# Interleaving the two halves of the split activations in the down projection of a decoder layer

## The chip, the cores and the metric

The kernel runs on one core of a Trainium2 chip. The metric is the device time of one execution in microseconds; the time of a kernel is the median over its runs. TensorE (PE) multiplies: a weight load puts a stationary operand of 128 x 128 into its array, and a matmul then streams a moving operand past it and accumulates into PSUM. VectorE (DVE), ScalarE (ACT) and GpSimd (POOL) work on elements; SyncE (SP) issues most transfers. All operands lie in SBUF, 128 partitions wide; what is said below of steps in bytes is within a partition.

## The reference

One decoder layer on 256 tokens of width 2048 in float32: a token mixer (mLSTM and RWKV-7 side by side), a cross-attention into 256 memory tokens, and a channel mixer, each with an RMS norm before and after and a residual. The change lies in the channel mixer:

```python
def conv_glu_ffn(h, w_up, conv_w, conv_b, w_down):
    u = h @ w_up
    uc = conv_b + sum(conv_w[j] * shift_right(u, CONV_WIDTH - 1 - j) for j in range(CONV_WIDTH))
    gate, up = split_cols(uc, (D_FF, D_FF))
    return (jax.nn.gelu(gate, approximate=True) * up) @ w_down
```

D_FF is 8192, so the last product is (256 x 8192) by (8192 x 2048). It is the last stage of the kernel, before the final norm and residual.

## The kernel before, in words

**Two halves for precision.** TensorE multiplies faster in the rounded type fp32r than in float32. To keep float32 accuracy each operand is split: the high half is the value rounded to fp32r, the low half is what the rounding left. A product is three matmuls: high x high, low x high, high x low. The weights arrive by DMA as pieces of 512 KB (128 x 1024 words, the tile `raw`); ScalarE casts a piece into `wh` (line 391) and VectorE subtracts to get `wl` (line 421). The class `Feed` (line 345) keeps these three steps ahead of the matmuls by fixed distances, with four buffers for each tile. Activations are split by the helper `split` (line 232), a cast on ScalarE and a subtraction on VectorE; through a recording wrapper these instructions all show line 66 in the profile. All matmuls but the transposes are issued at line 181.

**Two kinds of stage.** In an "fm" stage the weights are stationary and the activations move, 256 columns (all tokens) per matmul. In a "tm" stage the activations are stationary, 128 tokens at a time, and the weights move, 512 columns per matmul. The up projection is "fm" (32 blocks of 512 columns, line 1870). The down projection, the stage of the change, is "tm" (line 2006): two blocks n of 1024 output columns each, and for each block 64 steps k over D_FF, 128 rows of w_fd at a time. One k is one weight piece. For each k the four PSUM banks of a block (two halves of the tokens by two halves of the 1024 columns) get three matmuls each, twelve per k and 2 x 64 x 12 = 1536 in all, each with a weight load of its own:

```python
    def tm_products(o, t, c, wx, first, last):
        ...
        mm(o, xh[:, t], wh[:, c], start=first, stop=False)
        mm(o, xl[:, t], wh[:, c], start=False, stop=False)
        mm(o, xh[:, t], wl[:, c], start=False, stop=last)
```

Here `xh` and `xl` are the halves of the activations of one k, 128 x 256 words each, and `t` picks 128 of the 256 tokens.

**Where the halves come from.** The gated activations wait in SBUF as 64 tiles `ac` (`actile`, line 1816). `asplit` (line 1879) splits two of them, k and k + 1, into one tile `as` of 1024 words per partition. Two such tiles take turns (tags au0 and au1), the last pair has a third (bg0). `ax` (line 1894) hands the halves to the matmuls and calls `asplit` one pair ahead: while pair n is multiplied, pair n + 1 is split into the buffer that pair n - 1 has left. So the first cast of a pair waits for the matmuls of the pair before last. The first two pairs are split during the last block of the up projection. Since the activations don't depend on n, all 64 are split again for the second block: 128 casts and 128 subtractions. The last four k of the stage are taken bank by bank, all four k for one bank and then for the next, so that the output of the first banks can be finished while the last are still filled; their splits are issued before the first of those matmuls.

**Order of the work.** The program writes the order of each engine's instructions out by hand; `Spread` (line 71) deals the other work of VectorE and ScalarE out between the matmuls by a cost estimate that does not depend on steps in memory. Nothing in the order depends on the layout of `as`.

**Layout of `as` before.** The 1024 words of a partition are four rows of 256 tokens: high of k, high of k + 1, low of k, low of k + 1. Each half of each k lies contiguously, and a weight load reads 128 words in a row.

Of the kernel before, what the change touches and what calls it, by code (L numbers as in the profile page):

```python
# [145 lines left out]
def _layer(ctx, tc, nc, d, dbg):  # L146
# [21 lines left out]
    def C(name, tag, shape=None, dt=F32):  # L168
        return mp.tile(shape or [P, S], dt, tag=tag, bufs=1, name=name)
# [62 lines left out]
    def split(hi, lo, src):  # L232
        act.copy(hi, src)
        dve.tensor_sub(lo, src, hi)
# [1581 lines left out]
    def actile(k):  # L1816
        while len(M["ac"]) <= (k // 16 if k < 32 else 2 + (k - 32) // 8):
            n = len(M["ac"])
            M["ac"].append(big("ac") if n < 2 else U("ac"))
        return M["ac"][k // 16][:, k % 16] if k < 32 else M["ac"][2 + (k - 32) // 8][:, (k - 32) % 8]  # L1820
# [41 lines left out]
    def fu_xs(b):  # L1862
        def xs(k):
            if b == 31 and k == 12:
                asplit(0)
                asplit(2)
            return M["res"].tile(k)
        return xs
# [10 lines left out]
    def asplit(k):  # L1879

        if k not in M["as"]:
            n = k // 2
            if k == 126:
                a = C("as", "bg0", [P, 1024], F32R)
            else:
                a = mp.tile([P, 1024 + 128], F32R, tag=f"au{n % 2}", bufs=1, name="as")[:, 0:1024]
            a = a.rearrange("p (i j s) -> p i j s", i=2, j=2)
            a, b_ = a[:, 0], a[:, 1]
            for j in range(2):
                split(a[:, j], b_[:, j], actile((k + j) % 64))  # L1890
                M["as"][k + j] = (a[:, j], b_[:, j])
        return M["as"][k]

    def ax(n):
        def xs(k):
            kk = n * 64 + k
            if kk == 58:
                side.need(fu["task"])
            if kk == 24:
                load_gain()  # L1900
            if kk == 80:
                tables("natural_log_exp_and_others")
            if k % 2 == 0:
                asplit(kk)
                if kk + 2 < 128 and (k < 62 or n == 0):
                    asplit(kk + 2)
            return M["as"].pop(kk)
        return xs
# [192 lines left out]
```

## Time and profile before

| | |
|---|---|
| time, median of 3 runs | 1866.33 us (1866.29 to 1867.76) |
| profiled execution, first to last instruction (span) | 1863.2 us |
| median of the runs less that span | 3.1 us |
| granted TensorE clock, mean | 0.999 |
| busy: PE, PEld, DVE, ACT | 99%, 95%, 70%, 55% |
| up projection, settled part (from 938.94 us) | 568.50 us, 5016 matmuls |
| down projection (from 1507.44 us) | 348.20 us, 1536 matmuls |
| casts and subtractions into `as` | 128 of 404 ns, 128 of 421 ns |

The span is that of one execution taken by the profiler; the runs were timed without it, and include what lies before the first and after the last instruction. The profile lists instructions in groups ("out<-in", the shape, the count, then busy time in us, the mean of one in ns, and the idle time of the engine ahead of them with what ended it). PEld is the weight loads, which overlap the matmuls. A matmul's duration in the profile is a model that contains the pipeline, so that matmuls overlap in it; their rate is read from their starts. The chain of waits is the work followed back from the last instruction through whatever released each step.

### The profile page before, as it was taken

Reading aid. Unit: us, or ns where it says so; the run is one execution under the profiler, and the core shown is the slowest. Engines: PE = TensorE matmul, PEld = TensorE weight load, DVE = VectorE, ACT = ScalarE, POOL = GpSimd, SP = SyncE. Lnnn points to the kernel's source line nnn. Section 1 sums busy time; section 2 is a strip of 40 time slices with the busy share of each in tenths; the row PEclk is TensorE's granted clock in tenths of the full one; section 3 lists DMA queues with packets and bytes.
Section 4 is the critical chain, followed back from the end, with each engine's and each line's share of the span. In section 5 each row is a group of like instructions: output and inputs, shape, how many; then the busy total and the mean of one; then the engine's idle time right before and its main releaser. Section 6 shows DMA issues by size and latency. Waiting matters only on the chain.

```text
span 1863.2 us, 36212 instructions
## 1 busy us (share of the span) xinstructions
PE 1853.5 (99%) x14934; PEld 1767.5 (95%) x14934; DVE 1295.5 (70%) x1832; ACT 1017.0 (55%) x1492; POOL 32.4 (2%) x62
## 2 busy tenths in 40 slices
PE   9999999999999999999999999999999999999998
PEld 9999988999999999999999999999999988888887
DVE  7789777566675857787766667776666775556555
ACT  6876445655454646665554455444445554545544
POOL 0000020000000000000000000000000000000000
PEclk9999999999999999999999999999999999999999
DMA  7556544344555765555666666666666666666664
GB/s 261 186 166 203 180 149 160 136 160 158 172 195 196 277 197 180 165 180 172 202 192 194 196 195 196 185 194 199 195 194 195 197 192 215 194 193 192 194 192 145
DMA packets 98198, 351.47 MB, mean 189 GB/s; under 512 B 11056, under 2 KB 11568, under 8 KB 97648
## 3 DMA queue, kind: packets, MB, share of 16 engines
q1 hardware_dynamic: 97168, 348.01, 58.6%
q8 instruction: 117, 1.92, 0.4%
q10 hardware_dynamic: 864, 1.15, 0.2%
q14 instruction: 49, 0.40, 0.1%
HBM read 347.01 MB, written 2.10 MB: 187 GB/s over the span
## 4 chain that ended last, share of the span: by engine, by line
PE 98%; DVE 1%; DMA 0%; issue 0%; ACT 0%; ACTq 0%; DVEq 0%
PE fm L181 68%; PE tm L181 25%; PE gram L181 0%; DVE wl L421 0%; PE Y L181 0%; DMA w<-in_w_in_dram 0%; PE num L181 0%; PE lv L181 0%; DVE ql L66 0%; PE X L181 0%; PE U L181 0%; PE zg L181 0%; DVE z L66 0%; PE zwa L181 0%; PE xsc L181 0%
## 5 line engine op out<-in xcount | busy, mean ns | idle before, releaser
L421 DVE TENSOR_TENSOR wl<-raw,wh 128x1024 fp32r<-128x1024 f32 (+1 forms) x639 | 774.8, 1218 | 412.7 <-ACT wh L391 406.5
L391 ACT CAST wh<-raw 128x1024 fp32r<-128x1024 f32 (+1 forms) x639 | 663.6, 1043 | 476.0 <-PE fm L181 362.5
L181 PE MATMUL fm<-fh,wh 128*128 128x256 f32 x2048 | 564.2, 277 | 0.6 <-DVE fh L66 0.6
L181 PE MATMUL fm<-fh,wl 128*128 128x256 f32 x2048 | 563.2, 276 | 0.0
L181 PE MATMUL fm<-fl,wh 128*128 128x256 f32 x2048 | 563.2, 276 | 0.0
L181 PEld LDWEIGHTS fm<-fh,wh 128*128 128x128 f32 x2048 | 383.6, 188 | 0.8 <-DVE fh L66 0.8
L181 PEld LDWEIGHTS fm<-fl,wh 128*128 128x128 f32 x2048 | 383.5, 188 | 0.0
L181 PEld LDWEIGHTS fm<-fh,wl 128*128 128x128 f32 x2048 | 383.5, 188 | 0.0
L181 PE MATMUL tm<-wh,as 128*128 128x512 f32 x1024 | 315.1, 389 | 0.0
L181 PE MATMUL fm<-hh,wh 128*128 128x256 f32 x1024 | 284.3, 280 | 1.7 <-ACT wh L402 1.5
L181 PE MATMUL fm<-hl,wh 128*128 128x256 f32 x1024 | 281.7, 277 | 0.0
L181 PE MATMUL fm<-hh,wl 128*128 128x256 f32 x1024 | 281.5, 277 | 0.1
L181 PEld LDWEIGHTS tm<-wh,as 128*128 128x128 f32 x1024 | 192.2, 188 | 39.8
L181 PE MATMUL tm<-wl,as 128*128 128x512 f32 x512 | 199.2, 389 | 0.0
L181 PEld LDWEIGHTS fm<-hh,wh 128*128 128x128 f32 x1024 | 191.9, 188 | 3.4 <-ACT wh L402 1.7
L181 PEld LDWEIGHTS fm<-hl,wh 128*128 128x128 f32 x1024 | 191.9, 188 | 0.1
L181 PEld LDWEIGHTS fm<-hh,wl 128*128 128x128 f32 x1024 | 191.5, 188 | 0.3 <-DVE wl L421 0.3
L181 PEld LDWEIGHTS tm<-wl,as 128*128 128x128 f32 x512 | 96.1, 188 | 19.9
L66 ACT CAST as<-ac 128x256 fp32r<-128x256 f32 x128 | 45.6, 404 | 110.8 <-PE tm L181 110.8
L66 DVE TENSOR_TENSOR as<-ac,as 128x256 fp32r<-128x256 f32 x128 | 48.6, 421 | 61.7 <-ACT as L66 61.7
L181 PE MATMUL fm<-mgh,wh 128*128 128x256 f32 x256 | 70.9, 277 | 0.0
L181 PE MATMUL fm<-mgl,wh 128*128 128x256 f32 x256 | 70.8, 276 | 0.0
(406 smaller groups left out, 2225.0 us busy)
## 6 DMA issues: line engine op xcount, KB each, us to landing
raw<-in_w_fu_dram SPq DMA_DIRECT2D x256, 512.0 KB, 4.1
raw<-in_w_in_dram SPq DMA_DIRECT2D x152, 512.0 KB, 3.6
raw<-in_w_fd_dram SPq DMA_DIRECT2D x128, 512.0 KB, 3.9
raw<-in_w_br_dram SPq DMA_DIRECT2D x32, 512.0 KB, 4.1
raw<-in_w_mo_dram SPq DMA_DIRECT2D x32, 512.0 KB, 4.3
raw<-in_w_xk_dram SPq DMA_DIRECT2D x8, 512.0 KB, 4.2
raw<-in_w_xv_dram SPq DMA_DIRECT2D x8, 512.0 KB, 3.6
raw<-in_w_xq_dram SPq DMA_DIRECT2D x8, 512.0 KB, 4.0
```

Of the source, the lines that this page charges most:

```text
L66: return f(out, *a, **k)
L181: pe.matmul(out, lhsT, rhs, start=start, stop=stop, skip_group_check=True)
L391: nc.scalar.copy(wh, r)
L421: nc.vector.tensor_sub(wl, r, self.st[self.nl][0])
```

## The change

The view through which `asplit` cuts its tile into halves (i), the two k (j) and the tokens (s) is changed. Before, i is the outermost index of the 1024 words and s the innermost. After, j is outermost, then s, and i is innermost: for each k, the 512 words are high and low of token 0, high and low of token 1, and so on. The casts write, the subtractions read and write, and the weight loads read every second word, a step of 8 bytes. The tile, its place, its size, the instructions and their order are the same.

```diff
@@ -1884,7 +1884,7 @@
                 a = C("as", "bg0", [P, 1024], F32R)
             else:
                 a = mp.tile([P, 1024 + 128], F32R, tag=f"au{n % 2}", bufs=1, name="as")[:, 0:1024]
-            a = a.rearrange("p (i j s) -> p i j s", i=2, j=2)
+            a = a.rearrange("p (j s i) -> p i j s", i=2, j=2)
             a, b_ = a[:, 0], a[:, 1]
             for j in range(2):
                 split(a[:, j], b_[:, j], actile((k + j) % 64))
```

## The prediction

> **What bounds the kernel now.** I read the page first: engine shares, then the chain of waits.
>
> ```profile
> span 1863.2 us, 36212 instructions
> PE 1853.5 (99%) x14934; PEld 1767.5 (95%) x14934; DVE 1295.5 (70%) x1832; ACT 1017.0 (55%) x1492; POOL 32.4 (2%) x62
> PE 98%; DVE 1%; DMA 0%; issue 0%; ACT 0%; ACTq 0%; DVEq 0%
> PE fm L181 68%; PE tm L181 25%; PE gram L181 0%; DVE wl L421 0%; PE Y L181 0%; DMA w<-in_w_in_dram 0%; PE num L181 0%; PE lv L181 0%; DVE ql L66 0%; PE X L181 0%; PE U L181 0%; PE zg L181 0%; DVE z L66 0%; PE zwa L181 0%; PE xsc L181 0%
> ```
>
> The chain is TensorE for 98% of the span. The change touches only the stage that multiplies by w_fd, so next I took the chain in order of time (start, length, what). Its last long pieces are the up projection (256 moving columns per matmul) and the stage in question (512 columns):
>
> ```profile
> 938.94 568.50 PE fm L181 x5016
> 1507.44 348.20 PE tm L181 x1536
> ```
>
> The second piece is one unbroken run. 348.20 / 1536 = 226.7 ns per matmul; 568.50 / 5016 = 113.34 ns in the stage before. Twice 113.34 is 226.68, so the beat goes with the moving columns, 0.443 ns each, in both. Yet the 256-column stage makes one 128-column weight load per 113.34 ns and this one makes one per 226.7. Writing the beat as (columns x a + one load x b), b comes out as 2 x 113.34 - 226.69 = -0.01 ns: in the steady state a weight load costs the beat nothing.
>
> The stage's engine times, and the four groups that the change touches (busy us, mean ns of one, then idle time before):
>
> ```profile
> core 0: us, PE busy (x) PEld busy (x) DVE busy (x) ACT busy (x) POOL busy (x), PEclk, DMA share, GB/s
> 1507.40:1855.60 348.20, 348.20 (x1538) 288.37 (x1537) 212.01 (x275) 178.54 (x272) 0.00 (x0) 1.00 0.61 189
> L181 PEld LDWEIGHTS tm<-wh,as 128*128 128x128 f32 x1024 | 192.2, 188 | 39.8
> L181 PEld LDWEIGHTS tm<-wl,as 128*128 128x128 f32 x512 | 96.1, 188 | 19.9
> L66 ACT CAST as<-ac 128x256 fp32r<-128x256 f32 x128 | 45.6, 404 | 110.8 <-PE tm L181 110.8
> L66 DVE TENSOR_TENSOR as<-ac,as 128x256 fp32r<-128x256 f32 x128 | 48.6, 421 | 61.7 <-ACT as L66 61.7
> ```
>
> PE has no gap, its clock is 1.00, and VectorE and ScalarE are idle for 136 and 170 us of the 348. The stage can only become longer through TensorE's own beat, or if a split comes late.
>
> **The change part by part.** Nothing is added or removed: 128 casts, 128 subtractions, 1536 loads and as many matmuls remain, with no DMA or wait moved. Tile, size and buffer are the same; each pair of k values still fills its own 512 words per k. Three things read or write with another step.
>
> *The 1536 weight loads* read 128 words 8 bytes apart instead of 4. No load of the trace has a step above one word, so the price is bounded. What a load takes when nothing covers it is seen where the matmuls have a single moving column:
>
> ```profile
> 314.43 0.97 PEld L181 LDWEIGHTS den<-ones,pw 128*128 128x128 f32 x8
> ```
>
> Eight loads within 0.97 us, the last one 0.19 long (the 188 ns of the groups, which is thus a latency): (0.97 - 0.19) / 7 = 111 ns per load. In the changed stage a load has 226.7 ns until the next is due, so it is free up to 226.7 / 111 = 2.03 times its present time. The nearest rows with a large step are on VectorE, where one operation writes and reads with a step of 128 bytes (the tile comp, lines 932 to 983); beside it the same operation without a step:
>
> ```profile
> L983 DVE SCALAR_TENSOR_TENSOR comp<-gramA,con,comp 128x256 f32<-128x256 f32 x1 | 0.7, 716 | 0.0
> ...
> L66 DVE SCALAR_TENSOR_TENSOR ha<-haT,par,ha 128x256 fp32r<-128x256 f32 x8 | 3.7, 482 | 3.8 <-ACT ha L66 3.8
> ```
>
> A step sixteen times as wide as the new one costs 234 ns on 256 elements, 0.91 ns each, or 1.5 times in all. On a load's 128 words that would be 117 ns: 228 instead of 111, over the beat by 1.5 ns, or 1536 x 1.5 = 2.3 us. That is the upper end, since the new step is nearer to none; the lower end is 0, as a faster load shortens nothing (b above). I take 0. The cover is the matmul running meanwhile; without it the 117 ns would cost 1536 x 0.117 = 180 us.
>
> The Trainium skill (SBUF — State Buffer, the box on cachelines under "Door 1: The DMA port swizzle") gives lines of 16 bytes, full bandwidth from two hits per line on, and a penalty when each access crosses to another line. Four-byte words at a step of 8 bytes hit each line exactly twice, so by it the load stays at 111 ns, and a step of 16 would be the first to pay. The sum is 0 by it too, but the 2.3 us of the upper end and the second rival below would fall away. The 234 ns of the 128-byte row agree with its penalty; no row here has a step of 8.
>
> *The beat itself* can change where the loads' reads meet those of the running matmul. The trace knows a slower beat: the stage's first matmuls, two stretches of one form in the chain, and an earlier 512-column stage.
>
> ```profile
> 1507.28 0.63 PE L181 MATMUL tm<-wh,as 128*128 128x512 f32 x2
> ...
> 1508.66 0.61 PE L181 MATMUL tm<-wh,as 128*128 128x512 f32 x2
> ...
> 1509.34 0.61 PE L181 MATMUL tm<-wh,as 128*128 128x512 f32 x2
> ```
> ```profile
> 756.74 2.83 PE tm L181 x24
> 774.63 2.73 PE tm L181 x24
> ```
> ```profile
> 246.22 0.39 PE L181 MATMUL tm<-wh,hh 128*128 128x512 f32 x1
> ...
> 247.38 0.40 PE L181 MATMUL tm<-wl,hh 128*128 128x512 f32 x1
> ```
>
> From 1507.28 to 1508.66 there are six matmuls, 230 ns each; then three in 0.68 us, 226.7 each, and so to the end. In the chain, 24 matmuls of 256 columns take 2.83 us in one place and 2.73 in another: 117.9 against 113.8. At 246 us five steps take 1.16 us, 232.0 ns. The excess is 4 to 5 ns with 256 and with 512 columns, so it goes by matmul or load, not by column. Which reads meet in it the trace does not say. Bounds: if the first matmuls start on the fast beat, 6 x 3.3 ns = 0.02 us are gained; if all 1536 take 232.0, 1536 x 5.3 ns = 8.1 us are lost. I take 0, because the present loads leave the slow beat after six matmuls and more than 1500 follow without a relapse.
>
> The Trainium skill (TensorE: Matmul & The Clock Gate, "Step-by-step: what each phase is for") says that TensorE has two independent read ports, so that loading the next weights takes no bandwidth from the running matmul. By that rule the step of the loads cannot bring the slow beat, and this part is 0 as well. The long run at 226.7 agrees; what the beat of 232 is remains open by it, and I do not let the rule strike out the first rival.
>
> *The splits.* ScalarE writes the high half, VectorE reads it and writes the low half, now with a step of 8 bytes: 256 instructions. Lower end 0, upper end the 234 ns above for each, 256 x 0.234 = 60 us of work on two engines. What covers it, in a middle pair and in the last one:
>
> ```profile
> 1599.98 0.71 ACT L66 CAST as<-ac 128x256 fp32r<-128x256 f32 x2 [1.89 <-PE tm L181]
> 1605.42 0.41 ACT L66 CAST as<-ac 128x256 fp32r<-128x256 f32 x1 [1.89 <-PE tm L181]
> ...
> 1600.42 0.76 DVE L66 TENSOR_TENSOR as<-ac,as 128x256 fp32r<-128x256 f32 x2 [1.08 <-ACT as L66]
> ...
> 1842.80 0.70 ACT L66 CAST as<-ac 128x256 fp32r<-128x256 f32 x2
> 1844.07 0.75 DVE L66 TENSOR_TENSOR as<-ac,as 128x256 fp32r<-128x256 f32 x2
> 1845.94 0.62 PE L181 MATMUL tm<-wh,as 128*128 128x512 f32 x2
> ```
>
> A pair of k values takes 24 x 0.2267 = 5.44 us (1599.98 to 1605.42). ScalarE is released when the pair before has left the buffer, and VectorE has the low halves at 1601.18. They are read when the next pair begins, around the next release at 1605.4: some 4.2 us to spare, against at most four times 0.234 = 0.94 us more. The last pair is tightest: ready at 1844.82, first read at 1845.94 (the third k of the last four, after six matmuls from 1844.58), 1.1 us to spare. Behind them on ScalarE and VectorE wait the cast and subtraction of a weight piece, once per 2.72 us; a piece's share goes from (178.5 + 212.0) / 128 = 3.05 us on two engines to at most 3.5 of 5.4. I take 0. Without this cover it would be 60 us.
>
> **Sum.** 0 + 0 + 0. The profiled span stays 1863.2 us; the median of the runs, 1866.33, lies 3.1 us above that span, which the change does not touch. Forecast 1866.3 us.
>
> **Rivals.** *The slow beat stays through the stage* (the side that is slower). For it: the change alters just the loads' reads, and the excess goes by load or matmul. Against it: these addresses settle on the fast beat. It decides from a share of 46% of the matmuls on (3.7 of 8.1 us). Price 8.1 us: 1874.4. Chance 0.20.
>
> *The load takes more than 2.03 times 111 ns.* At three times, 334 ns, the beat grows by 107 ns: 1536 x 0.107 = 165 us, 2031 us. For it: no row shows a load with a step. Against it: 128 bytes of step only reach 2.05 times by the VectorE row. That one load becomes several instructions (the change not being what it says) belongs here and would show as a count above 1536. Chance 0.05.
>
> *The splits come late.* 60 us at most, 1926 us; against it the 1.1 and 4.2 us to spare. Chance 0.02.
>
> *Faster.* The load's part of the beat is nil, and the start is worth 0.02 us; a gain needs a beat under 0.443 ns per column, which no matmul of this form shows in two stages of 5016 and 1536. Chance 0.03.
>
> **How the numbers follow.** No change 0.70; faster 0.03; slower 0.20 + 0.05 + 0.02 = 0.27, where 0.2% (3.7 us) is about what this kernel's measurement can tell. The range goes from 1864, a little under the runs shown (1866.29 to 1867.76), to 1876, the first rival with that spread of 1.5 us; it leaves out the last three cases, 0.10. The likeliest case alone: 1864 to 1869.
>
> **What would show it.** Right: the piece "PE tm" of 1536 at 348.2 us. Slow beat: about 356 us, steps of 232 ns. Load bound: steps well above 232, loads with no idle time ahead of them. Splits: the cast and subtraction above 404 and 421 ns show the step's price there, and idle time of PE before the first matmul of a pair would show them late. A piece below 347 us, or a difference outside this stage, would make the reasoning wrong.

## The result, and the profile after

The changed kernel takes 1875.53 us (median of 4 runs, 1874.2 to 1878.6) against 1866.31 us; the ratio is 1.0053 with a 95% interval of 1.0038 to 1.0067. It is slower: the medians lie 9.2 us apart, and the ratio makes it 9.9 us. The forecast was no change, 1866.3 us; what happened has the form of the prediction's first rival, a slower beat through the whole stage.

The span, and the two last long pieces of the chain of waits of the changed kernel (start, length, what):

```profile
span 1876.8 us, 36212 instructions
```
```profile
942.41 568.50 PE fm L181 x5016
1510.91 358.42 PE tm L181 x1536
```

The number of instructions is the same. The up projection is as long as before to the last digit. The down projection has grown from 348.20 to 358.42 us: 10.22 us, which accounts for the whole measured loss within its interval. 358.42 / 1536 = 233.3 ns per matmul instead of 226.7. The profiled span grew by 13.6 us, but 3.5 of them lie ahead of 942.41 us, where nothing was changed; in the other kernels below, whose code is also the same up to there, that piece starts anywhere from 937.41 to 941.17 us. This part is left out from here on, and each kernel is read by its piece of 1536 matmuls.

The start of the stage in order of time, and a point far into it (start, length, engine and so on, matmuls that overlap in the profile merged):

```profile
1510.74 0.64 PE L181 MATMUL tm<-wh,as 128*128 128x512 f32 x2
1511.22 0.39 PE L181 MATMUL tm<-wl,as 128*128 128x512 f32 x1
1511.45 0.63 PE L181 MATMUL tm<-wh,as 128*128 128x512 f32 x2
...
1700.22 0.39 PE L181 MATMUL tm<-wl,as 128*128 128x512 f32 x1
1700.45 0.63 PE L181 MATMUL tm<-wh,as 128*128 128x512 f32 x2
1700.92 0.39 PE L181 MATMUL tm<-wl,as 128*128 128x512 f32 x1
```

From 1700.22 to 1700.92 there are three matmuls in 0.70 us. Before, the stage left a beat of 230 ns after six matmuls; now all 1536 stay on 233.3. The stage's engines and its groups:

```profile
core 0: us, PE busy (x) PEld busy (x) DVE busy (x) ACT busy (x) POOL busy (x), PEclk, DMA share, GB/s
1510.90:1869.30 358.40, 358.40 (x1538) 296.45 (x1537) 212.14 (x275) 178.07 (x272) 0.00 (x0) 1.00 0.60 184
```
```profile
L181 PEld LDWEIGHTS tm<-wh,as 128*128 128x128 f32 x1024 | 197.6, 193 | 41.1
...
L66 DVE TENSOR_TENSOR as<-ac,as 128x256 fp32r<-128x256 f32 x128 | 48.7, 422 | 68.1 <-ACT as L66 68.0
L66 ACT CAST as<-ac 128x256 fp32r<-128x256 f32 x128 | 46.6, 419 | 116.4 <-PE tm L181 116.3
```

PE is busy without a gap at a clock of 1.00. The loads still have 40 ns of idle time each ahead of them (41.1 us over 1024), so they don't fill the beat. The subtraction is as fast as before (422 ns against 421), the cast 15 ns slower (419 against 404), and ScalarE waits longer for PE than before (116.4 us against 110.8): the splits are not what the stage waits for. What is left is the beat.

### The profile page after: what moved, and what is told of

It reads as the page before. It is cut to its first block, busy times and chain, and to the rows that moved or that the text cites. A ratio compares the mean times of both kernels' runs of the same rounds, so it can differ in the third digit from the quotient of the medians.

```text
span 1876.8 us, 36212 instructions
## 1 busy us (share of the span) xinstructions
PE 1867.3 (99%) x14934; PEld 1779.2 (95%) x14934; DVE 1295.5 (69%) x1832; ACT 1016.8 (54%) x1492; POOL 32.4 (2%) x62
## 4 chain that ended last, share of the span: by engine, by line
PE 99%; DMA 0%; DVE 0%; ACT 0%; ACTq 0%; issue 0%; DVEq 0%
PE fm L181 69%; PE tm L181 26%; PE gram L181 0%; PE Y L181 0%; DMA w<-in_w_in_dram 0%; PE num L181 0%; PE lv L181 0%; PE X L181 0%; PE U L181 0%; PE zg L181 0%; PE xsc L181 0%; PE zwa L181 0%; PE xt L1920 0%; PE Tn L181 0%; PE stb L181 0%; PE xo L181 0%
## 5 line engine op out<-in xcount | busy, mean ns | idle before, releaser
L181 PE MATMUL tm<-wh,as 128*128 128x512 f32 x1024 | 321.0, 394 | 0.0
L181 PEld LDWEIGHTS tm<-wh,as 128*128 128x128 f32 x1024 | 197.6, 193 | 41.1
L66 ACT CAST as<-ac 128x256 fp32r<-128x256 f32 x128 | 46.6, 419 | 116.4 <-PE tm L181 116.3
```

Source lines behind the costliest of these rows:

```text
L66: return f(out, *a, **k)
L181: pe.matmul(out, lhsT, rhs, start=start, stop=stop, skip_group_check=True)
```

## The experiments

Theory A after the result: a load that steps 8 bytes costs its matmul 6.7 ns, wherever its words lie. Theory B: load and moving operand are read at the same time, and how their reads meet is decided by layout and place of both; the change only moved the stage out of a favourable pattern. Theory C: the load got longer and sets the beat itself.

### Step of 8 bytes without the neighbourhood

```diff
-            a = a.rearrange("p (j s i) -> p i j s", i=2, j=2)
+            a = a.rearrange("p (i s j) -> p i j s", i=2, j=2)
```

> The step of 8 bytes is kept, but high and low halves lie 2 KB apart again: the words of k and k + 1 alternate instead. Theory A (a stepped load costs its matmul a fixed time, whatever lies between its words): the beat of the last stage stays at 233.3 ns, the piece of 1536 matmuls at 358.4 us. Theory B (the neighbourhood of high and low, or another place of the reads, brings back the slow beat known from before): the beat is back at 226.7 ns, the piece at 348.2 us.

The chain of waits of this kernel:

```profile
1506.66 358.42 PE tm L181 x1536
```

The same length to the last digit. That high and low halves lie next to each other isn't needed for the loss; the step is enough, in this place.

### Step of 16 bytes

```diff
-            a = a.rearrange("p (j s i) -> p i j s", i=2, j=2)
+            a = a.rearrange("p (s j i) -> p i j s", i=2, j=2)
```

> All four rows of the tile alternate word by word, so that each load steps 16 bytes. Theory A, in the form that a load pays 0.83 ns for each 64 bytes more that it reaches over (8 more of them gave 6.7 ns, 24 more give 20): beat 246.7 ns, piece 378.9 us. Theory B (a beat with two states, fast and slow): 233 ns or 226.7 ns, piece 358 or 348 us. Theory C (the load itself gets longer and sets the beat once it no longer fits): with a single word used of each 16 bytes the load at least doubles, 222 ns or more, and the beat is the load's own length, anywhere above 233 ns.

```profile
1505.91 361.09 PE tm L181 x1536
```
```profile
L181 PEld LDWEIGHTS tm<-wh,as 128*128 128x128 f32 x1024 | 278.8, 310 | 0.0
...
L66 DVE TENSOR_TENSOR as<-ac,as 128x256 fp32r<-128x256 f32 x128 | 76.8, 652 | 83.0 <-ACT as L66 82.8
L66 ACT CAST as<-ac 128x256 fp32r<-128x256 f32 x128 | 72.8, 674 | 117.4 <-PE tm L181 117.4
```

361.09 / 1536 = 235.1 ns. A price for every further 64 bytes is refuted: 246.7 was expected of it. Two beats alone, theory B as it was put here, miss it by 1.8 ns. The loads now have no idle time ahead of them, which is theory C for this step; the sections below give 233.3 ns for a load at 16 bytes, so they alone nearly fill this beat. The same step costs the cast 270 ns (674 against 404) and the subtraction 231 (652 against 421). Together they are busy for 149.6 us instead of 94.2, and these 55 us more still hide.

### Only the high halves stepped

```diff
-            a = a.rearrange("p (j s i) -> p i j s", i=2, j=2)
-            a, b_ = a[:, 0], a[:, 1]
+            a, b_ = a[:, 0:512].rearrange("p (s j) -> p j s", j=2), a[:, 512:1024].rearrange("p (j s) -> p j s", j=2)
```

> Only the high halves are stepped (the words of k and k + 1 alternate), the low halves lie in a row: two loads of three step 8 bytes. Theory A (each stepped load costs its matmul 6.7 ns, a contiguous one nothing): a mean beat of 226.7 + 2/3 x 6.7 = 231.1 ns, the piece of 1536 matmuls at 355.0 us. Theory B (the reads of loads and moving operand meet in a repeating pattern which the layout and the place of both decide together): no price per load; a mean anywhere from 226.7 to 233.3 ns.

```profile
1507.25 358.41 PE tm L181 x1536
```

Theory A expected 355.0 us and falls: with a third of the loads contiguous again the stage costs the same. It is not a sum over loads.

### Moving the other operand: 64 and 192 bytes

The weight pieces of the last stage are placed later in their buffers, in `staged`. First the changed layout with 64 bytes (16 words; its edit is shown), then, with `o = 48`, the layout of before and the changed one with 192 bytes:

```diff
             o = 0 if c >= 512 and self.kind[i] == "tm" else 16
+            if c == 1024:
+                o = 16
```

> The changed layout, with the moving operand (the weight pieces of the last stage) placed 64 bytes later in its buffer. Theory A: unchanged, 233.3 ns and 358.4 us. Theory B: the meeting of loads and moving reads is another, so the beat leaves 233.3 ns, most likely to 226.7.

> The layout of before, without any step; only the weight pieces of the last stage lie 192 bytes later in their buffers. Theory A: nothing steps, so the beat is 226.7 ns and the piece 348.2 us. Theory B, with the number that the sections of bare matmuls gave for this offset: 233.3 ns, 358.4 us, as much as the change itself cost.

> The changed layout with the weight pieces 192 bytes later. Theory A: unchanged at 233.3 ns, 358.4 us. Theory B, from the same sections: 230.0 ns, 353.3 us.

One row of the chain of waits from each, in this order (one execution of each):

```profile
1507.45 358.42 PE tm L181 x1536
```
```profile
1508.12 358.40 PE tm L181 x1536
```
```profile
1509.67 353.30 PE tm L181 x1536
```

With 64 bytes the mean did not move, against what I expected of theory B, though the steps became uneven (230 to 236 ns in turn instead of 233 each). The second kernel decides: no load steps, the layout is that of before, and the stage is as long as after the change. The third has the stepped loads and is 5.1 us shorter than the changed kernel. Both lengths had been foretold by the sections below.

The second kernel was also timed in several runs:

> The layout of before with all weight pieces of the last stage 192 bytes later, now timed against the kernel before. Theory B: 358.4 us in the last stage and a ratio of 1.005, as for the change. If the step were needed for the loss: 1.000.

```profile
1505.97 358.40 PE tm L181 x1536
```

Its ratio to the kernel before is 1.0053 (1.0038 to 1.0068; 1873.82 us against 1864.73). Displacing the weights by 192 bytes, with contiguous loads, costs as much as the change did.

### TensorE alone

Sections of 96 matmuls on one stationary and two moving tiles, in the order of the stage, and nothing on the other engines. In between stand two float32 matmuls of one column, which the profile shows as four:

```python
VIEW = {1: "p (i j s) -> p i j s", 2: "p (j s i) -> p i j s", 4: "p (s j i) -> p i j s"}
...
def section(n, step, off):
    ...
    v = st[:, 0:1024].rearrange(VIEW[step], i=2, j=2)
    ...
    for i, w in ((0, 0), (1, 0), (0, 1)):
        mm(q[:, 0:n], v[:, i, j, t], mv[w][:, c:c + n], k == 0, k == 95)
```

> Only TensorE works here, on one stationary tile and two moving tiles, and the layer is left out (the output is zero). Sections of 96 matmuls of 512, 256, 128 and 32 moving columns, each with loads of step 4, 8 and 16 bytes; then 512 columns with the moving operand 64, 128 and 192 bytes later, steps 4 and 8. Theory A: 226.7, 233.3 and 246.7 ns with 512 columns at any offset; with 256 columns 113.3, 120 and 133; the time of a bare load (32 columns) about 111 ns at every step or a few ns more. Theory B: the beat depends on the offset, not on the step. Theory C: the bare load is visibly longer, 118 ns or more at 8 bytes and above 222 ns at 16, and the 256-column beat follows it.

From its chain of waits, sections of 256 and 128 columns (the number after "step" counts words of 4 bytes):

```profile
78.83 11.62 PE n256step1off L152 x96
...
90.79 11.63 PE n256step2off L152 x96
...
102.75 22.52 PE n256step4off L152 x96
...
125.61 10.78 PE n128step1off L152 x96
...
136.78 11.37 PE n128step2off L152 x96
```

With 128 moving columns, which at 0.443 ns each would take 57 ns, the load is the bound: 111.7 ns for a contiguous load, 117.8 at 8 bytes (means over a section's starts; 10.78 / 96 and 11.37 / 96 contain its first step). So the step of 8 bytes does lengthen the load, by 6 ns or 5%, far inside its 226.7. At 16 bytes a load is 233.3 ns (22.52 us for 256 columns, at a granted clock of 1.00), 2.09 times; with 512 columns this step has a beat of 235.0 ns, as in the kernel. With 256 columns, steps of 4 and 8 bytes run alike, at 120 ns: here contiguous loads have the excess as well, against 113.3 in the up projection. The sections of 32 columns ran at a granted clock of 0.50 and can't be compared with these. One thing shows in them all the same: steps of 4 and 8 bytes take 213.3 ns there, but 16 bytes take 233.3, as at a clock of 1.00, so the length of the 16-byte load did not follow the clock.

The second set of sections:

> TensorE alone again (the layer is left out, the output is zero). 512 columns at eight offsets of the moving operand, 64 bytes apart, steps 4 and 8. Theory B: the beat depends on offset and step together and comes back every 256 bytes (226.7, 229.0, 232.5, 233.3 for step 4; 233.3, 233.3, 231.4, 230.0 for step 8). Theory A: flat in the offset. Then loads of a single repeated word (step 0) and loads of 64 columns instead of 128: if the excess comes from the lines that a load fetches, step 0 stays at 226.7 ns or below at any offset, and 64 columns have at most half of the excess, 230.0 ns. Last, bare loads under 128 columns with steps of 4, 8, 12, 16 and 32 bytes: by two words per 16-byte line being enough, 112, 118, then more, with 233 ns from 16 bytes on and no further rise at 32.

Some rows of its chain of waits; "off" counts words by which the moving tiles are displaced, "w64" is a load of 64 columns:

```profile
33.20 22.51 PE n512step2off0x L152 x96
...
146.75 22.51 PE n512step1off48x L152 x96
...
169.60 22.21 PE n512step2off48x L152 x96
...
373.35 22.35 PE w128step0off0x L152 x96
...
396.03 21.91 PE w128step1off0x L152 x96
...
531.67 22.24 PE w64step2off0x L152 x96
...
576.97 21.85 PE w64step2off48x L152 x96
```

A section contains one longer step after the four matmuls ahead of it, so the beat is taken from the starts of its last 48 matmuls and the one before them, in ns:

| moving operand displaced by | contiguous loads | step 8 bytes |
|---|---|---|
| 0 and 256 bytes | 226.7 | 233.3 |
| 64 and 320 | 228.9 | 233.3 |
| 128 and 384 | 232.4 | 231.5 |
| 192 and 448 | 233.3 | 230.0 |

The beat of a section depends on step and place together and repeats every 256 bytes, as theory B had it. The two numbers at 192 bytes, times 1536, are 358.4 and 353.3 us: the two kernels above. What I had thought of the mechanism fell, though. A load that reads one and the same word 128 times has 231.7 ns at both offsets tried, and loads of 64 columns have 230.0 and 232.7 contiguous, 231.1 and 226.7 at 8 bytes, displaced by 0 and 192 bytes. The excess does not follow the number of lines or words that a load fetches. (The last three bare sections, with steps of 12, 16 and 32 bytes, ran at half the clock and are not read, so what I expected of 12 and 32 bytes is untested.)

Is there a place where 8 bytes run at 226.7?

> TensorE alone (the layer is left out, the output is zero), 512 columns. Is there a place of the two moving tiles at which loads of 8-byte step run at 226.7 ns? Twelve offsets that are no multiple of 64 bytes, then all unequal pairs of offsets 0, 64, 128 and 192 bytes for the tile that plays the high and the one that plays the low half of the weights, then the stationary tile moved by 64, 128 and 192 bytes with steps 4 and 8. Theory B (the pattern of meetings decides, the step has no price of its own): at least one of the 27 places with step 8 lies within 1 ns of 226.7, and moving the stationary tile acts like moving the moving one the other way round (step 4: 233.3, 232.5, 229.0). Against it (8 bytes always meet more often): none below 230.0 ns.

```profile
307.55 22.09 PE n512step2off0low32base0x L152 x96
...
488.83 22.10 PE n512step2off48low0base0x L152 x96
...
556.18 22.50 PE n512step1off0low0base16x L152 x96
...
692.26 21.93 PE n512step1off0low0base0x L152 x96
```

None of the 27 was within 1 ns; the best, four of those where the two moving tiles lie differently, have 228.9. So that part of the expectation failed: among the places tried, stepped loads of 128 columns are never quite clear. Moving the stationary tile does act like moving the other operand back: 64, 128 and 192 bytes gave 233.3, 232.4 and 228.9 with contiguous loads, which are the table's values for 192, 128 and 64. Over all sections of 512 columns with steps of 4 and 8 bytes no settled beat lay outside 226.7 to 233.3 ns.

### The best of these places in the kernel

```diff
             o = 0 if c >= 512 and self.kind[i] == "tm" else 16
+            if c == 1024:
+                o = 48 if name == "wh" else 0
```

> The changed layout; in the last stage the high halves of the weights lie 192 bytes later, the low halves as before, one of the best places that the bare sections gave for a step of 8 bytes (228.9 ns). Theory B: beat 228.9 ns, piece 351.6 us, 3.4 us over the kernel before: a ratio near 1.002. If the step itself had a price per load: 233.3 ns, 358.4 us, ratio 1.005.

```profile
1506.87 351.61 PE tm L181 x1536
```

351.61 us, as foretold from the sections, and a ratio of 1.0016 (1.0007 to 1.0026) to the kernel before. With the stepped loads of the change in place, two thirds of its cost in the stage (6.8 of 10.2 us) are gone by moving the weights' high halves 192 bytes.

## Why the prediction was wrong, point by point

*What bounds the kernel.* Right: the loss is TensorE's own beat in the stage, 6.65 ns x 1536 = 10.2 us. The bare sections show the same two beats with no other engine at work, so none is needed for it.

*"in the steady state a weight load costs the beat nothing"* True only of the pattern it was worked out from. Both stages compared had their operands in favourable places; with the same contiguous loads the beat is 6.7 ns longer when the weights lie 192 bytes further. The two equations gave a property of a place, and I read it as one of loads. The kernel's code could have raised the question: `staged` starts "tm" pieces of 512 or more columns at the head of their buffers and the others 64 bytes later, and a table `KICK` moves 19 single pieces. It gives no reason, and the prediction asks for none.

*The loads' length.* Right, with a bound too wide: 6 ns on 111 at 8 bytes, not up to 117, and the loads still have idle time ahead of them. The Trainium skill's rule (SBUF — State Buffer, the box on cachelines under "Door 1: The DMA port swizzle"), that two hits per 16-byte line are enough, agrees nearly: 1.05 times at 8 bytes, 2.09 at 16. It answers the length of the load, not the beat.

*The beat itself.* This is the step that failed: "I take 0, because the present loads leave the slow beat after six matmuls and more than 1500 follow without a relapse." The run of the present loads could not speak for loads that read other addresses in the same time. With the changed loads all 1536 matmuls stay on 233.3 ns, and the term put at 0 is 10.2 us. The rival had 0.20, and its price, 8.1 us at 232.0 ns, was too low. That 1875.5 us lies inside the stated range of 1864 to 1876 is in part luck: the range ended 1.5 us above a price that was 2.1 us too small.

The rows behind the term say less than the prediction took from them. It sets two stretches of 24 matmuls side by side, at 117.9 and 113.8 ns, as if each had a beat of its own. The same stretches in the kernel after and in the kernel with only the high halves stepped, whose code is the same up to there:

```profile
757.72 2.73 PE tm L181 x24
775.51 2.73 PE tm L181 x24
```
```profile
755.57 2.82 PE tm L181 x24
773.61 2.83 PE tm L181 x24
```

Neither stretch keeps its beat. In the ten traces of the layer the first, read by its starts, runs at 117.8 ns in eight and at 113.3 in two, the second at 113.3 in seven and at 117.8 in three, with unchanged code, places and a clock of 1.00. So in short stretches something besides step and place picks the beat, and these rows could not tell which one the changed loads would get. In the long runs this was not seen: the places measured more than once gave the same settled beat each time, in the stage and in the sections, though the stage is entered from other matmuls.

*The rule on ports.* The Trainium skill (TensorE: Matmul & The Clock Gate, "Step-by-step: what each phase is for") says that loading the next weights takes no bandwidth from the running matmul. The runs don't fit this: with nothing but TensorE at work, 512 columns take 226.7 or 233.3 ns by where the two operands lie, so load and running matmul do affect each other. Whether it is bandwidth that is lost, they don't show. It was right not to strike the rival out by the rule.

*The splits.* Right that they hide. The price at 8 bytes is 15 ns on the cast and 1 on the subtraction; the 234 ns taken from the 128-byte row come in at 16 bytes, and even then hide.

*The other rivals.* The load over 2.03 times its length came only at 16 bytes. Nothing became faster.

Shown is that the settled beat depends on step and relative place of stationary and moving operand, with a period of 256 bytes. That reads meet is the picture behind theory B, and not shown; the load of a single repeated word, which is not clear either, speaks against a simple count of lines or words. Open are why a step of 8 bytes found no clear place and what makes a short stretch take one beat or the other in the same place; other distances than those listed weren't tried.

## What to carry to other kernels

A matmul's beat that looks like a floor can be a floor of one arrangement: before changing how a stationary operand is laid out, measure the beat in a few dozen bare matmuls with the loads and the moving operand at their real distance modulo 256 bytes, which here foretold the stage within 0.1%. A slower beat anywhere in the trace for the same form of matmul is a price that the change may switch on for a whole stage; compare it over several executions first, as a short stretch can show either beat. When operands are moved, read the beat again even if no access pattern has changed.

## What the runs showed of the hardware that was not expected

- With contiguous operands only, a displacement of the moving operand by 192 bytes costs 3% of every matmul of 512 columns (226.7 to 233.3 ns), and 256 bytes bring it back.
- A load of one repeated word is not cheaper for the running matmul: 231.7 ns, more than a contiguous load in a clear place.
- A load of 128 words takes 111.7, 117.8 and 233.3 ns at steps of 4, 8 and 16 bytes, the last also at half the clock; ScalarE's cast of 256 words 404, 419 and 674 ns, VectorE's subtraction 421, 422 and 652 ns.
- The same 24 matmuls of 256 columns, with code and places unchanged, run at 113.3 ns in some executions and at 117.8 in others, and nowhere in between.
